# Inverse square roots as a POOL power, and four re-ordered places, in a one-core hybrid decoder trunk

## The chip, the cores and the metric

The kernel runs on one core of a Trainium2 chip. The metric is the device time of one execution in microseconds (us). TensorE (PE) does the products, VectorE (DVE), ScalarE (ACT) and GpSimd (POOL) the rest; transfers are issued from the queues of SP (SyncE), ACT and POOL.

## What is computed

Two residual layers over x of 512 tokens by 1024 features, all in float32, each layer followed by a dense squared-ReLU MLP of width 4096, and an RMSNorm at the end:

```python
for i in range(2):
    h = rmsnorm(x, norm_mix_g[i])
    h = chunked_spatial_gating(h, ...) if i == 0 else retention(h, ...)   # mixers A and B
    x = x + h
    h = rmsnorm(x, norm_ffn_g[i])
    x = x + squared_relu_mlp(h, mlp_w1[i], mlp_w2[i])
return rmsnorm(x, final_norm_g)
# rmsnorm(x, g) = x * rsqrt(mean(x*x, -1) + 1e-6) * g
```

Mixer A has one more RMSNorm over its gate half v, mixer B one for each of its four heads. So an inverse square root of a mean of squares is taken at ten places: nine times for all 512 tokens at once, as a 128x4 tile, and in the last norm for four groups of 128 tokens, each a 128x1 tile.

## The kernel before, in words

**Products.** Every float32 factor is split into a high part (a cast to the type fp32r) and a low part (the rest); a product is three passes on PE: high by high, high by low, low by high (`mm3`, L261). Weights come in as raw tiles by DMA from SP (some MLP tiles get a second matrix added by a DMA from POOL, L199). A raw tile holds two pieces; for each piece ACT casts `wH` (L220) and DVE subtracts `wL` (L227). `refill` (L246) issues this two to three pieces ahead of the products.

**Order.** The kernel writes the order out by hand: each engine executes its instructions in the order in which the program emits them. `steps` is a list of functions, one for each weight piece, run at the end (L1148). Small work is slipped behind a piece by `behind` hooks. A norm is a generator (`norm`, L348) whose stages such hooks advance: first the split of the sum of squares `ssq` into a high part on ACT and a low part on POOL (L316, L317); then two products with a matrix of ones (L325, L326), a masked sum on DVE (L329 to L331) and `rsqrt` (L295), eleven small DVE instructions, which give `r4`; then the split and spreading of `r4` over a row, and a last product that broadcasts it (L343 to L346).

**Start.** Five products of the identity with itself (L1140) come first, then the columns of the norm gains, then `x_chunk` (L449) for chunks 0 and 1 of x: four transposes into one PSUM tile, the casts of the first weight piece (L1145, L1146), `hH` (L457), `hL` (L459), and a copy to `xT` (L460). Then `v0` (L599) runs the first 512 columns of v with accumulators in four PSUM tiles of the tag `acc` (six tiles; the tag `mis` has two): for each chunk k three groups of four products (hH by wH, hH by wL, hL by wH; L619). Further chunks of x are transposed between them (`two_chunks`, L591). At its last piece (i == 3) the first norm's split is issued ahead of chunk 6's products, and its two statistics products ahead of chunk 7's. `tokens` (L394) runs the other three parts of v.

**MLP.** `dense` (L804) runs up to 4096 features in four quarters; for three of them the down products (`seven`, L719) follow, named p in a string that orders them. The last quarter's activations are split by `split_a` (L706), four at a time, the second four behind the sixth of the seven products of the third quarter (L820). Layer 0's last down quarter is `down_last` (products named dn, L840), layer 1's is the pair of `tokens` calls at L1121 (products named dt).

**End.** The last half of columns (c = 1) ends token group by token group (`ends`, L1081): twelve products for each of four groups, then `evac_last` (L1046): an add on DVE, squares with their sum on ACT, and a multiplication by the gain on POOL. `finish` (L1057) is a generator: the mean on DVE, an inverse root in eleven small DVE instructions, interleaved with the next group's work by `go`, then the two halves of the output, one on ACT (L1076), one on DVE (L1078), each followed by a DMA from SP (L1077, L1079).

Of the kernel before, what the change touches and what calls it, by code (L numbers as in the profile page):

```python
# [88 lines left out]
def trunk(ctx, tc, x, norm_mix_g, norm_ffn_g, a_w_in, a_b_in, a_v_norm_g, a_w_s, a_b_s, a_w_out,  # L89
# [48 lines left out]
    ms0 = keep.tile([P, NT], F32, name="ms0")  # L138

    keep.tile([P, 328], F32, name="fill")  # L140
# [4 lines left out]
    nc.gpsimd.memset(rows, 1.0)  # L145

# [148 lines left out]
    def rsqrt(dst, a, n, name):  # L295

        y, t = [work.tile([P, n], F32, tag=f"rs{i}_{n}", name=f"{name}_{i}", bufs=2) for i in range(2)]
        nc.vector.tensor_scalar(out=t.bitcast(I32), in0=a.bitcast(I32), scalar1=1, scalar2=None, op0=ALU.logical_shift_right)
        nc.vector.tensor_scalar(out=y.bitcast(I32), in0=t.bitcast(I32), scalar1=-1.0, scalar2=float(0x5F3759DF - (1 << 31)), op0=ALU.mult, op1=ALU.add)
        for i in range(3):  # L300
            nc.vector.tensor_mul(t, y, y)
            nc.vector.scalar_tensor_tensor(out=t, in0=t, scalar=0.5, in1=a, op0=ALU.mult, op1=ALU.mult)
            nc.vector.scalar_tensor_tensor(out=dst if i == 2 else y, in0=t, scalar=1.5, in1=y, op0=ALU.subtract, op1=ALU.mult)
# [16 lines left out]
    def stats(ssq, dst, scale, name):  # L320

        hi, lo = split(ssq, f"st_{name}", nc.gpsimd)
        yield
        ps = mis(f"st_{name}")
        nc.tensor.matmul(ps, lhsT=onesr, rhs=hi, start=True, stop=False)  # L325
        nc.tensor.matmul(ps, lhsT=onesr, rhs=lo, start=False, stop=True)  # L326
        own = tmp(f"own_{name}", "uz")
        a = work.tile([P, NT], F32, tag="ms", name=f"ms_{name}", bufs=2)
        nc.vector.tensor_tensor(out=by_token(own), in0=by_token(ps), in1=diag_mask, op=ALU.mult)  # L329
        nc.vector.tensor_reduce(out=a, in_=by_token(own), op=ALU.add, axis=mybir.AxisListType.X)  # L330
        nc.vector.tensor_scalar(out=a, in0=a, scalar1=scale, scalar2=EPS, op0=ALU.mult, op1=ALU.add)  # L331
        rsqrt(dst, a, NT, f"rs_{name}")
        yield
# [60 lines left out]
    def tokens(plist, bufs, evac, name, behind=None, last=None):  # L394

        accs = {}
        behind = behind or {}

        def one(i):
            def run(p):  # L400
                if i == 0:
                    for n in range(NT):
                        accs[n] = acc(f"{name}_{n}")
                aH, aL = bufs()
                for n in range(NT):
                    s = slice(n * P, (n + 1) * P)
                    for k in range(2):
                        kk = 2 * i + k
                        mm3(accs[n], aH[kk][:, s], aL[kk][:, s], p.hi[:, k, :], p.lo[:, k, :], kk == 0, kk == 7)
                advance()  # L410
                refill()
                if i in behind:
                    behind[i]()
                if i == 3:
                    for n in range(NT):
                        launch(evac(n, accs[n]))
            return run

        for i, p in enumerate(plist[:2] if last else plist):
            step(one(i), p)  # L420
        if last:
            step(lambda *ps: last(bufs, accs, evac, *ps), *plist[2:])
# [75 lines left out]
    def v_stats():  # L498
# [4 lines left out]
        rsqrt(rs4, a, NT, "rs_v")  # L503
# [94 lines left out]

    def v0(i):  # L599
        def run(p):  # L600
# [5 lines left out]
            for k in range(2):  # L606
# [3 lines left out]
                if i == 3:  # L610
                    prep(5 + k)
                    if k == 0:
                        squares(6, MIX)
                        squares(7, MIX)
                    next(nrm)
                wh, wl = p.hi[:, k, :], p.lo[:, k, :]
                for j, (h, w) in enumerate(((hH, wh), (hH, wl), (hL, wh))):
                    for n in range(NT):
# [3 lines left out]
            if i == 3:  # L622
                for n in range(NT):
                    launch(evac_v(0)(n, accs0[n]))
                next(nrm)
# [4 lines left out]
    tokens(vl[1], hs, evac_v(1), "v1", {1: nxt(nrm)})  # L630
    tokens(vl[2], hs, evac_v(2), "v2", {1: ws_prep})
# [172 lines left out]
    def dense(l, hooks):  # L804
# [6 lines left out]
        for q in range(3):  # L811
# [4 lines left out]
            for what in "upupupupuupuupp" if q == 2 else "upupupupupupupu":  # L816
                if what == "p":
                    products[j]()
                    j += 1
                    if q == 2 and j == 6:  # L820
# [225 lines left out]
    def evac_last(c):  # L1046
        def ev(n, ps):
# [5 lines left out]
            nc.gpsimd.tensor_tensor(out=xv, in0=xv, in1=wide[:, 512 * c : 512 * (c + 1)], op=ALU.mult)  # L1053
# [3 lines left out]
    def finish(n):  # L1057


        a = [work.tile([P, 1], F32, tag=f"fa{i}", name=f"fa{i}_{n}", bufs=2) for i in range(3)]  # L1060
        t, y = [work.tile([P, 1], F32, tag=f"fy{i}", name=f"fy{i}_{n}", bufs=2) for i in range(2)]
        nc.vector.scalar_tensor_tensor(out=a[0], in0=ssf[:, n, 1:2], scalar=1.0 / D, in1=ms0[:, n : n + 1], op0=ALU.mult, op1=ALU.add)
        yield
        nc.vector.tensor_scalar(out=t.bitcast(I32), in0=a[0].bitcast(I32), scalar1=1, scalar2=None, op0=ALU.logical_shift_right)
        nc.vector.tensor_scalar_mul(a[1], a[0], 0.25)
        nc.vector.tensor_scalar_mul(a[2], a[0], 0.0625)
        yield
        nc.vector.tensor_scalar(out=y.bitcast(I32), in0=t.bitcast(I32), scalar1=-1.0, scalar2=float(0x5F3759DF - (1 << 31)), op0=ALU.mult, op1=ALU.add)
        yield
        for i in range(3):  # L1070
            nc.vector.scalar_tensor_tensor(out=t, in0=y, scalar=a[i], in1=y, op0=ALU.mult, op1=ALU.mult)
            yield
            nc.vector.scalar_tensor_tensor(out=y, in0=t, scalar=3.0, in1=y, op0=ALU.subtract, op1=ALU.mult)
            yield
        o = [zt(f"out0{n}"), z2t(f"out1{n}")]
        nc.scalar.activation(o[0], tok[0][:, n, :], AF.Copy, scale=y)  # L1076
        nc.sync.dma_start(out=out[0, n * P : (n + 1) * P, 0:512], in_=o[0])  # L1077
        nc.vector.tensor_scalar_mul(o[1], tok[1][:, n, :], y)  # L1078
        nc.sync.dma_start(out=out[0, n * P : (n + 1) * P, 512:1024], in_=o[1])  # L1079

    def ends(bufs, accs, evac, *ps):  # L1081

        aH, aL = bufs()
        fins = []

        def go(steps):
            for _ in range(steps):
                for g in list(fins):
                    if next(g, "end") == "end":
                        fins.remove(g)  # L1090

        for n in range(NT):
# [6 lines left out]
            go(5)  # L1099
            fins.append(finish(n))  # L1100
            go(4 if n < 2 else 0)
        go(16)
# [10 lines left out]
    def load_gain():  # L1113
        nc.sync.dma_start(out=wide, in_=final_norm_g.partition_broadcast(P))
        nc.vector.tensor_scalar_mul(wide, wide, 0.125)
# [22 lines left out]
    warm = mis("warm")  # L1138
    for _ in range(5):
        nc.tensor.matmul(warm[:, 0:P], lhsT=ident, rhs=ident, start=True, stop=True)  # L1140
    columns(rows2, 0, 16)
    prep_tiles(0)
    for k in range(2):
        p = order[0]
        x_chunk(k, [lambda: nc.scalar.copy(out=p.hi[:, k, :], in_=p.raws[0].tile[:, k, :]),  # L1145
                    lambda: nc.vector.tensor_sub(out=p.lo[:, k, :], in0=p.raws[0].tile[:, k, :], in1=f32(p.hi[:, k, :]))])  # L1146
# [50 lines left out]
```

## Time and profile before

| | us |
|---|---|
| median of 3 runs (lowest, highest) | 1380.65 (1379.38, 1381.09) |
| the profiled execution's own time | 1382.22 |
| its span, first to last instruction | 1380.5 |
| PE busy in it | 1363.5 (99%) |
| DVE, ACT, POOL busy | 877.5, 567.3, 158.0 |

The profile is of one execution; its starts are in us from the span's start. A row of the timeline gives the start, the length, the engine, the line, the operation, output and inputs with their shapes, how many instructions are merged into the row, and in brackets how long the engine was idle before it and what ended that. A PE row's length holds the drain of the pipeline, so products overlap: their pace is read from the starts.

### The profile page before, as it was taken

Reading aid. Unit: us, or ns where it says so; the run is one execution under the profiler, and the core shown is the slowest. Engines: PE = TensorE matmul, PEld = TensorE weight load, DVE = VectorE, ACT = ScalarE, POOL = GpSimd, SP = SyncE. Lnnn points to the kernel's source line nnn. Section 1 sums busy time; section 2 is a strip of 40 time slices with the busy share of each in tenths; the row PEclk is TensorE's granted clock in tenths of the full one; section 3 lists DMA queues with packets and bytes.
Section 4 is the critical chain, followed back from the end, with each engine's and each line's share of the span. In section 5 each row is a group of like instructions: output and inputs, shape, how many; then the busy total and the mean of one; then the engine's idle time right before and its main releaser. Section 6 shows DMA issues by size and latency. Waiting matters only on the chain.

```text
span 1380.5 us, 15485 instructions
## 1 busy us (share of the span) xinstructions
PE 1363.5 (99%) x6180; PEld 1132.1 (82%) x6180; DVE 877.5 (64%) x1228; ACT 567.3 (41%) x812; POOL 158.0 (11%) x122
## 2 busy tenths in 40 slices
PE   8999999999999999999999999999999999999997
PEld 6888888888888888788888888888888888888875
DVE  6847756675665756676656574474594665766655
ACT  4647634334444434422333432333234544434342
POOL 3010111130100000011112100100121000100002
PEclk9999999999999999999999999999999999999999
DMA  6232222234684748233222222131127376665621
GB/s 230 93 127 71 92 92 92 92 123 139 164 208 131 200 136 183 93 117 111 69 85 63 90 92 92 61 121 62 62 92 214 92 183 182 144 192 150 155 77 61
DMA packets 115800, 166.71 MB, mean 121 GB/s; under 512 B 2880, under 2 KB 67984, under 8 KB 115472
## 3 DMA queue, kind: packets, MB, share of 16 engines
q1 hardware_dynamic: 103024, 140.55, 31.0%
q0 software_dynamic: 12672, 25.17, 10.8%
q8 instruction: 48, 0.79, 0.2%
q14 instruction: 24, 0.20, 0.0%
q10 hardware_dynamic: 32, 0.01, 0.0%
HBM read 163.62 MB, written 2.10 MB: 120 GB/s over the span
## 4 chain that ended last, share of the span: by engine, by line
PE 96%; DVE 2%; POOL 1%; ACT 0%; issue 0%; DVEq 0%; POOLq 0%; ACTq 0%
PE up L264 24%; PE g L264 6%; PE ro L264 6%; PE vv L264 6%; PE qk L264 6%; PE u L264 6%; PE o L264 6%; PE v L264 5%; PE dt L264 3%; PE dn L264 2%; PE av L264 2%; PE sm11a L264 2%; PE sm10a L264 2%; PE sm01a L264 2%; PE sm00a L264 2%; PE sm12a L264 1%
## 5 line engine op out<-in xcount | busy, mean ns | idle before, releaser
L227 DVE TENSOR_TENSOR wL<-raw,wH 128x1024 fp32r<-128x1024 f32 x235 | 300.5, 1283 | 48.9 <-issue 13.8
L220 ACT CAST wH<-raw 128x1024 fp32r<-128x1024 f32 x235 | 244.3, 1045 | 79.0 <-PE dt L264 14.3
L264 PE MATMUL up<-hH,wH 128*128 128x512 f32 x480 | 187.2, 390 | 0.2 <-ACT xtok L1042 0.2
L264 PE MATMUL up<-hL,wH 128*128 128x512 f32 x480 | 186.8, 389 | 0.0
L264 PE MATMUL up<-hH,wL 128*128 128x512 f32 x480 | 186.8, 389 | 0.0
L696 ACT ACTIVATE aF<-r 128x512 f32<-128x512 f32 x54 | 34.2, 633 | 218.2 <-DVE r L695 218.2
L695 DVE SCALAR_TENSOR_TENSOR r<-up,wide 128x512 f32<-128x512 f32 x54 | 37.4, 692 | 128.5 <-PE up L264 120.0
L264 PEld LDWEIGHTS up<-hH,wH 128*128 128x128 f32 x480 | 90.1, 188 | 19.1 <-ACT xtok L1042 0.5
L264 PEld LDWEIGHTS up<-hH,wL 128*128 128x128 f32 x480 | 90.1, 188 | 18.8
L264 PEld LDWEIGHTS up<-hL,wH 128*128 128x128 f32 x480 | 90.1, 188 | 18.7
L199 POOL DMA_DIRECT2D raw<-in_mlp_w_dram x22 | 28.7, 1306 | 391.1 <-DVE wL L227 261.1
L293 POOL TENSOR_TENSOR ssq<-ssq,sq 128x512 f32<-128x512 f32 x28 | 43.0, 1537 | 162.2 <-ACT sq L292 161.9
L227 DVE TENSOR_TENSOR wL<-more,wH 128x1024 fp32r<-128x1024 f32 x40 | 48.7, 1219 | 6.2 <-issue 4.7
L264 PE MATMUL u<-hH,wH 128*128 128x512 f32 x128 | 50.6, 395 | 0.0
L264 PE MATMUL g<-hH,wH 128*128 128x512 f32 x128 | 50.5, 395 | 0.0
L264 PE MATMUL o<-yH,wH 128*128 128x512 f32 x128 | 50.4, 394 | 0.0
L264 PE MATMUL ro<-ryL,wH 128*128 128x512 f32 x128 | 50.0, 391 | 0.0
L264 PE MATMUL qk<-hH,wH 128*128 128x512 f32 x128 | 50.0, 391 | 0.0
L264 PE MATMUL vv<-wH,hH 128*128 128x512 f32 x128 | 50.0, 391 | 0.0
L264 PE MATMUL ro<-ryH,wH 128*128 128x512 f32 x128 | 50.0, 390 | 0.0
L264 PE MATMUL ro<-ryH,wL 128*128 128x512 f32 x128 | 50.0, 390 | 0.0
L264 PE MATMUL g<-hH,wL 128*128 128x512 f32 x128 | 49.9, 390 | 0.0
(394 smaller groups left out, 3087.2 us busy)
## 6 DMA issues: line engine op xcount, KB each, us to landing
raw<-in_mlp_w_dram SPq DMA_DIRECT2D x50, 1024.0 KB, 5.2
raw<-in_b_w_in_dram SPq DMA_DIRECT2D x24, 1024.0 KB, 5.1
raw<-in_mlp_w_dram POOLq DMA_DIRECT2D x22, 1024.0 KB, 9.1
more<-in_mlp_w_dram SPq DMA_DIRECT2D x20, 1024.0 KB, 5.1
raw<-in_a_w_in_dram SPq DMA_DIRECT2D x14, 1024.0 KB, 5.1
raw<-in_a_w_out_dram SPq DMA_DIRECT2D x8, 1024.0 KB, 5.0
raw<-in_b_w_out_dram SPq DMA_DIRECT2D x8, 1024.0 KB, 5.0
raw<-in_a_w_in_dram SPq DMA_DIRECT2D x8, 256.0 KB, 6.6
```

The costliest lines, as they stand in the source:

```text
L199: nc.gpsimd.dma_start(out=r.tile, in_=src, accum_op=ALU.add)
L220: nc.scalar.copy(out=p.hi, in_=p.src)
L227: nc.vector.tensor_sub(out=p.lo, in0=p.src, in1=f32(p.hi))
L264: nc.tensor.matmul(ps, lhsT=a, rhs=b, start=start and i == 0, stop=stop and i == 2, skip_group_check=resumed)
L293: nc.gpsimd.tensor_tensor(out=state["ssq"], in0=state["ssq"], in1=sq, op=ALU.add)
L695: nc.vector.scalar_tensor_tensor(out=r, in0=ps, scalar=0.0, in1=rbc, op0=ALU.max, op1=ALU.mult)
L696: nc.scalar.activation(a, r, AF.Square)
```

## The change

- `rsqrt` becomes one POOL instruction: the tile to the power of a tile `mhalf` that holds -0.5.
- The second chunk's transposes, casts and copies (`first_chunk(1)`) are issued behind the first four products of chunk 0 instead of ahead of them; two more products of the identity follow the first chunk's transposes.
- In `v0`'s last piece the split of the first norm is issued ahead of chunk 7's products, and the statistics products behind them. The second part of v takes two of its accumulators from `mis`, and the broadcast of `r4` moves behind the third part's first piece.
- The second `split_a` of a layer moves behind the seventh product.
- At the end the c = 1 half is no longer multiplied by the gain on POOL: one DVE instruction takes the sum, the root and the gain together. Its DMA goes from SP, that of the other half from ACT. Each group's way out is issued whole behind its products. The gain's multiplication by 0.125 goes.

```diff
+    mhalf = keep.tile([P, NT], F32, name="mhalf")
-    keep.tile([P, 328], F32, name="fill")
+    keep.tile([P, 320], F32, name="fill")
+    nc.gpsimd.memset(mhalf, -0.5)
...
-    def rsqrt(dst, a, n, name):
-        y, t = [work.tile([P, n], F32, tag=f"rs{i}_{n}", name=f"{name}_{i}", bufs=2) for i in range(2)]
...
-        for i in range(3):
-            nc.vector.tensor_mul(t, y, y)
...
+    def rsqrt(dst, a, n):
+        nc.gpsimd.tensor_tensor(out=dst, in0=a, in1=mhalf[:, 0:n], op=ALU.pow)
...
-    def tokens(plist, bufs, evac, name, behind=None, last=None):
+    def tokens(plist, bufs, evac, name, behind=None, last=None, banks=(acc,) * 4):
...
-                        accs[n] = acc(f"{name}_{n}")
+                        accs[n] = banks[n](f"{name}_{n}")
...
+    def first_chunk(k):
+        p = order[0]
+        x_chunk(k, [lambda: nc.scalar.copy(out=p.hi[:, k, :], in_=p.raws[0].tile[:, k, :]),
+                    lambda: nc.vector.tensor_sub(out=p.lo[:, k, :], in0=p.raws[0].tile[:, k, :], in1=f32(p.hi[:, k, :]))])
...
                     if k == 0:
                         squares(6, MIX)
                         squares(7, MIX)
-                    next(nrm)
+                    else:
+                        next(nrm)
                 for j, (h, w) in enumerate(((hH, wh), (hH, wl), (hL, wh))):
+                    if kk == 0 and j == 1:
+                        first_chunk(1)
...
             if i == 3:
+                next(nrm)
                 for n in range(NT):
                     launch(evac_v(0)(n, accs0[n]))
                 next(nrm)
...
-    tokens(vl[1], hs, evac_v(1), "v1", {1: nxt(nrm)})
-    tokens(vl[2], hs, evac_v(2), "v2", {1: ws_prep})
+    tokens(vl[1], hs, evac_v(1), "v1", banks=(acc, acc, mis, mis))
+    tokens(vl[2], hs, evac_v(2), "v2", {0: nxt(nrm), 1: ws_prep})
...
-                    if q == 2 and j == 6:
+                    if q == 2 and j == 7:
                         do(lambda: [split_a(l, i) for i in range(4, 8)])
...
             if c == 0:
                 nc.vector.tensor_scalar(out=ms0[:, n : n + 1], in0=ssf[:, n, 0:1], scalar1=1.0 / D, scalar2=EPS, op0=ALU.mult, op1=ALU.add)
-            nc.gpsimd.tensor_tensor(out=xv, in0=xv, in1=wide[:, 512 * c : 512 * (c + 1)], op=ALU.mult)
+                nc.gpsimd.tensor_tensor(out=xv, in0=xv, in1=wide[:, 0:512], op=ALU.mult)
...
     def finish(n):
+        a, y = [work.tile([P, 1], F32, tag=f"f{i}", name=f"f{i}_{n}", bufs=2) for i in "ay"]
+        nc.vector.scalar_tensor_tensor(out=a, in0=ssf[:, n, 1:2], scalar=1.0 / D, in1=ms0[:, n : n + 1], op0=ALU.mult, op1=ALU.add)
+        rsqrt(y, a, 1)
         o = [zt(f"out0{n}"), z2t(f"out1{n}")]
+        nc.vector.scalar_tensor_tensor(out=o[1], in0=tok[1][:, n, :], scalar=y, in1=wide[:, 512:D], op0=ALU.mult, op1=ALU.mult)
+        nc.sync.dma_start(out=out[0, n * P : (n + 1) * P, 512:1024], in_=o[1])
         nc.scalar.activation(o[0], tok[0][:, n, :], AF.Copy, scale=y)
+        nc.scalar.dma_start(out=out[0, n * P : (n + 1) * P, 0:512], in_=o[0])
...
     def load_gain():
         nc.sync.dma_start(out=wide, in_=final_norm_g.partition_broadcast(P))
-        nc.vector.tensor_scalar_mul(wide, wide, 0.125)
...
+    warm_up(5)
     columns(rows2, 0, 16)
     prep_tiles(0)
+    first_chunk(0)
+    warm_up(2)
```

The eleven-instruction chain of `finish`, its generator steps and the loop over chunks 0 and 1 ahead of `steps` go.

## Rows read from the trace of the kernel before

**Rows 1.** The page's first part: busy time, share of the span, instructions.

```profile
PE 1363.5 (99%) x6180; PEld 1132.1 (82%) x6180; DVE 877.5 (64%) x1228; ACT 567.3 (41%) x812; POOL 158.0 (11%) x122
```

**Rows 2.** Waits of PE, longest first: waiter, releaser, us, times, longest.

```profile
PE xt L452 <- DVE hL L459: 2.2, 1, 2.2
...
PE up L264 <- ACT xtok L1042: 0.2, 1, 0.2
```

**Rows 3.** Timeline of the start: PE, DVE and ACT around the first two chunks.

```profile
4.06 1.11 PE L452 MATMUL xt<-ident,xr 128*128 128x128 f32 x4
...
5.22 0.75 DVE L457 TENSOR_SCALAR hH<-xt,gT 128x512 fp32r<-128x512 f32 x1 [0.87 <-PE xt L452]
...
7.32 0.59 ACT L460 COPY xT<-xt 128x512 f32<-128x512 f32 x1 [1.89 <-DVE hL L459]
...
7.37 1.09 PE L452 MATMUL xt<-ident,xr 128*128 128x128 f32 x4 [2.19 <-DVE hL L459]
...
8.11 2.06 PE L619 MATMUL v<-wH,hH 128*128 128x512 f32 x4
...
9.96 1.91 PE L619 MATMUL v<-wL,hH 128*128 128x512 f32 x4
...
13.20 1.03 PE L452 MATMUL xt<-ident,xr 128*128 128x128 f32 x8
```

**Rows 4.** DMA issues from 1.8 to 2.0 us (chunk 1 of x, issued at 1.83): KB, landing.

```profile
xr<-in_x_dram SPq DMA_DIRECT2D x1, 256.0 KB, 5.4
```

**Rows 5.** Timeline of the first statistics: PE's last groups of chunk 6, the split, chunk 7.

```profile
30.82 1.07 PE L619 MATMUL v<-wL,hH 128*128 128x512 f32 x4
...
31.73 1.07 PE L619 MATMUL v<-wH,hL 128*128 128x512 f32 x4
...
32.95 1.28 POOL L317 TENSOR_TENSOR st_mix<-ssq,st_mix 128x512 fp32r<-128x512 f32 x1 [0.73 <-ACT st_mix L316]
...
34.28 0.50 PE L326 MATMUL st_mix<-st_mix,onesr 128*128 128x512 f32 x1 [0.86 <-POOL st_mix L317]
...
34.62 1.08 PE L619 MATMUL v<-wH,hH 128*128 128x512 f32 x4
```

**Rows 6.** Timeline at the end of layer 0's seventh product: the late splits, dn's first products.

```profile
580.38 2.49 DVE L714 TENSOR_TENSOR aL<-aF,aH 128x512 fp32r<-128x512 f32 x4
...
582.93 0.39 PE L264 MATMUL dn0a<-aL,wH 128*128 128x512 f32 x1
...
584.05 0.50 PE L264 MATMUL dn0a<-aH,wL 128*128 128x512 f32 x1 [0.74 <-DVE wL L227]
```

**Rows 7.** Timeline of the same place in layer 1: dt's first products.

```profile
1325.27 0.39 PE L264 MATMUL dt<-wH,aH 128*128 128x512 f32 x1
...
1326.58 0.50 PE L264 MATMUL dt<-wL,aH 128*128 128x512 f32 x1 [0.93 <-DVE wL L227]
```

**Rows 8.** Timeline of the end: first group's add and mean, last group's add, last DMA.

```profile
1362.05 0.69 DVE L1049 TENSOR_TENSOR xtok<-xtok,dt 128x512 f32<-128x512 f32 x1 [7.11 <-PE dt L264]
...
1363.59 0.16 DVE L1062 SCALAR_TENSOR_TENSOR fa<-ssf,ms 128x1 f32<-128x1 f32 x1 [0.85 <-ACT fsq L1050]
...
1370.21 0.69 DVE L1049 TENSOR_TENSOR xtok<-xtok,dt 128x512 f32<-128x512 f32 x1
...
1377.05 0.39 SPq L1079 DMA_DIRECT2D out_dram<-out  x1
```

**Rows 9.** Groups of POOL instructions by line and shape: busy us, mean ns, idle before.

```profile
L1053 POOL TENSOR_TENSOR xtok<-xtok,wide 128x512 f32<-128x512 f32 x8 | 10.3, 1286 | 81.4 <-ACT fsq L1050 81.4
...
L477 POOL TENSOR_SCALAR vgh<-gT 128x16 f32<-128x16 f32 x1 | 0.2, 243 | 0.0
```

**Rows 10.** Timeline: a three-operand DVE instruction on SBUF tiles of 128x512.

```profile
14.98 0.75 DVE L284 SCALAR_TENSOR_TENSOR hL<-xT,gT,hH 128x512 fp32r<-128x512 f32 x1
```

**Rows 11.** Timeline, POOL and DVE at layer 0's MLP norm: queued DMA, root's last instruction.

```profile
318.62 1.46 POOL L199 DMA_DIRECT2D raw<-in_mlp_w_dram  x1 [10.90 <-DMA raw<-in_mlp_w_dram]
...
318.76 0.16 DVE L303 SCALAR_TENSOR_TENSOR r<-rs_ffn,rs_ffn 128x4 f32<-128x4 f32 x1
```

More of the change, by code (lines that the diff above doesn't have):

```diff
@@ L293, in squares @@
             nc.gpsimd.tensor_tensor(out=state["ssq"], in0=state["ssq"], in1=sq, op=ALU.add)
-    def rsqrt(dst, a, n, name):
-        y, t = [work.tile([P, n], F32, tag=f"rs{i}_{n}", name=f"{name}_{i}", bufs=2) for i in range(2)]
-        nc.vector.tensor_scalar(out=t.bitcast(I32), in0=a.bitcast(I32), scalar1=1, scalar2=None, op0=ALU.logical_shift_right)
-        nc.vector.tensor_scalar(out=y.bitcast(I32), in0=t.bitcast(I32), scalar1=-1.0, scalar2=float(0x5F3759DF - (1 << 31)), op0=ALU.mult, op1=ALU.add)
-        for i in range(3):
-            nc.vector.tensor_mul(t, y, y)
-            nc.vector.scalar_tensor_tensor(out=t, in0=t, scalar=0.5, in1=a, op0=ALU.mult, op1=ALU.mult)
-            nc.vector.scalar_tensor_tensor(out=dst if i == 2 else y, in0=t, scalar=1.5, in1=y, op0=ALU.subtract, op1=ALU.mult)
+    def rsqrt(dst, a, n):
+        nc.gpsimd.tensor_tensor(out=dst, in0=a, in1=mhalf[:, 0:n], op=ALU.pow)
     def over_tokens(v):
@@ L331, in stats @@
         nc.vector.tensor_scalar(out=a, in0=a, scalar1=scale, scalar2=EPS, op0=ALU.mult, op1=ALU.add)
-        rsqrt(dst, a, NT, f"rs_{name}")
+        rsqrt(dst, a, NT)
         yield
@@ L502, in v_stats @@
         nc.vector.tensor_scalar(out=a, in0=s, scalar1=0.25 / GW, scalar2=EPS, op0=ALU.mult, op1=ALU.add)
-        rsqrt(rs4, a, NT, "rs_v")
+        rsqrt(rs4, a, NT)
         nc.vector.tensor_scalar_mul(rs4, rs4, 0.5)
@@ L1057, in finish @@
     def finish(n):
[L1060 to L1074, printed above, removed]
+        a, y = [work.tile([P, 1], F32, tag=f"f{i}", name=f"f{i}_{n}", bufs=2) for i in "ay"]
+        nc.vector.scalar_tensor_tensor(out=a, in0=ssf[:, n, 1:2], scalar=1.0 / D, in1=ms0[:, n : n + 1], op0=ALU.mult, op1=ALU.add)
+        rsqrt(y, a, 1)
         o = [zt(f"out0{n}"), z2t(f"out1{n}")]
+        nc.vector.scalar_tensor_tensor(out=o[1], in0=tok[1][:, n, :], scalar=y, in1=wide[:, 512:D], op0=ALU.mult, op1=ALU.mult)
+        nc.sync.dma_start(out=out[0, n * P : (n + 1) * P, 512:1024], in_=o[1])
         nc.scalar.activation(o[0], tok[0][:, n, :], AF.Copy, scale=y)
-        nc.sync.dma_start(out=out[0, n * P : (n + 1) * P, 0:512], in_=o[0])
-        nc.vector.tensor_scalar_mul(o[1], tok[1][:, n, :], y)
-        nc.sync.dma_start(out=out[0, n * P : (n + 1) * P, 512:1024], in_=o[1])
+        nc.scalar.dma_start(out=out[0, n * P : (n + 1) * P, 0:512], in_=o[0])
     def ends(bufs, accs, evac, *ps):
         aH, aL = bufs()
[L1084 to L1090, printed above, removed]
         for n in range(NT):
@@ L1098, in ends @@
             launch(evac(n, accs[n]))
[L1099 to L1102, printed above, removed]
+            finish(n)
     tt = {2: [(0, 0), (0, 1)], 3: [(0, 2)], 4: [(0, 3)], 5: [(1, 0)], 6: [(1, 1)], 7: [(1, 2), (1, 3)]}
@@ L1136, in trunk, with warm_up @@
     load_a()
-    warm = mis("warm")
-    for _ in range(5):
-        nc.tensor.matmul(warm[:, 0:P], lhsT=ident, rhs=ident, start=True, stop=True)
+    def warm_up(n):
+        warm = mis("warm")
+        for _ in range(n):
+            nc.tensor.matmul(warm[:, 0:P], lhsT=ident, rhs=ident, start=True, stop=True)
+    warm_up(5)
     columns(rows2, 0, 16)
     prep_tiles(0)
[L1143 to L1146, printed above, removed]
+    first_chunk(0)
+    warm_up(2)
     pos["piece"] = pos["low"] = raws[0].split = 1
```

## The prediction, on record before the changed kernel ran

> **What bounds the kernel now.** The page's first part first: PE is busy for 99% of the span, DVE for 64%, ACT for 41%, POOL for 11% [rows 1]. So a shorter instruction on DVE, ACT or POOL is worth nothing by itself; it counts where PE stands still, or before PE's first and behind PE's last product. The waits of PE come next: six entries in all, of which the longest is 2.2 us, at the start, and the shortest 0.2 us [rows 2]. PE's ends are modelled, so I then read the starts in the timeline, where a stall shows as a gap above the usual pace: four 128x512 products start 0.91 us after the four before (30.82 to 31.73, [rows 5]), 0.2275 us each, 2.73 us for a group of twelve and 5.46 us for a piece of 24. Four places stand out, and the change touches each.
>
> **The start.** Chunk 0's transposes start at 4.06, its hH is written at 5.22 + 0.75 = 5.97, and PE's next instruction, chunk 1's transposes, starts at 7.37 [rows 3]. The releaser shown is hL, but chunk 1 of x, issued at 1.83, landed 5.4 us later at 7.2 [rows 4]: either alone would hold PE. From 8.11 the first four products take 1.85 us (to 9.96), and the eight after them 3.24 us (to 13.20): 0.46 and 0.41 us each, about half the pace of rows 5 (1.2 GHz for 2.4), though the granted clock of the view reads full there. PE had worked at half pace, then idled before 7.37.
>
> The change puts the first four products ahead of chunk 1's transposes. Chunk 0's transposes end at 5.2, two more identity products fill about 1 us (estimate: the transposes' 0.27 us for each of their four passes), so the four start at about 6.2. They end at 8.05 at half pace. Chunk 1's transposes then wait for nothing new: x landed at 7.2; if they take the PSUM tile of chunk 0, they wait for its copy to xT, 7.32 + 0.59 = 7.91 [rows 3]. At half pace throughout (transposes 1.09, eight products 3.24) the next transposes start at 12.4 instead of 13.20: 0.8 us gained. At full pace from the first product on (transposes 8.0 to 8.5, eight at 0.2275) they start at 10.3: 2.9 us. Between them the pace doubles at about 9 us: 8.05 + 1.09 + 1.82 = 11.0, **2.2 us**, which I take, since PE now works without the pause of 5.2 to 7.4 and the old kernel, restarted at 7.4, doubled its pace by 13.2. The Trainium skill (TensorE: Matmul & The Clock Gate, Part 1) says that half rate is the default and that sustained work releases the clock; by that rule the unbroken work from the warm-up on would release it earlier and the term would lie near 2.9, by the rows alone it may stay at 0.8. Trace and rule agree on the half pace at the start. Behind this point hH, hL and weights of chunk 1 follow its transposes as before, with nothing else queued between.
>
> **The first statistics.** Chunk 6's products end at 31.73 + 0.91 = 32.64 on PE's pace; chunk 7's start at 34.62, because the low half of the split is written on POOL until 32.95 + 1.28 = 34.23 [rows 5]. Of the 1.98 us the two statistics products need 2 x 0.2275. Behind chunk 7's products (2.73 us) they find the split done: 32.64 + 2.73 = 35.4 against 34.23. **1.5 us** go. If POOL's chain does not move forward with the start, the margin of 1.1 us shrinks by the 2.2 gained there, and up to 1 us stays. Late next is r4, and with it the evacuation of the four first accumulators. The next part no longer waits for these (two tiles of acc, two of mis, the second of which DVE's masked sum frees 0.7 us behind the statistics); the third part asks for them four pieces, 21.8 us, later. On DVE the evacuation holds the third piece's wL: from the statistics to its end stand eight passes over 512 columns at 0.69 [rows 8], wL itself, twice as wide, 1.4, and small ones, some 0.8, together 7.7 us, against the two pieces that are ready, 10.9: the power may take 3.2 us there.
>
> **The late splits.** At layer 0's first dn products the starts go 582.93, 584.05: 1.12 - 0.23 = **0.9 us** lost to wL, which stands on DVE behind four subtractions of 2.49 us from 580.38 [rows 6]. In layer 1, the first product starts at 1325.27 and the second, the first that reads wL, at 1326.58: 1.31 - 0.23 = **1.1 us** [rows 7]. Moved behind the seventh product, the four leave wL 2.5 us earlier, more than either stall. What they feed comes late next: dn's second half of chunks starts 24 products, 5.46 us, after the seventh product; before it DVE has two adds of 0.69 [rows 8] and the 2.49, 3.9 us. A margin of 1.5 us; in layer 1 it is a piece more. No DMA moves with this step.
>
> **The end.** Before: the last group's add starts at 1370.21, the last DMA is issued at 1377.05 [rows 8], and the span ends 3.45 us later, at 1380.5. After: for each group, add, squares and mean take 1363.59 + 0.16 - 1362.05 = 1.70 us [rows 8], then the power p with 0.07 us of handing over on either side (estimate from the steps between engines in rows 5 and 8), then the three-operand product, 0.75 [rows 10], and 0.03: 2.62 + p. All are in order on DVE, so the next group's add stands behind this group's wait for POOL. PE gives a group every 2.73 us, so for p over 0.1 this loop sets the end: last issue at 1362.05 + 3 x (2.62 + p) + 1.70 + 0.14 + p + 0.75 + 0.05 = 1372.55 + 4p. The other half (ACT, with its DMA now from ACT) runs beside it. No row shows a power. The nearest below is POOL's smallest arithmetic, 0.243 us for 128x16, the nearest above its ordinary pass over 128x512, 1.286 [rows 9]: 1373.5 to 1377.7, a gain of 3.5 or a loss of 0.7. With one to four elements it is nearer to the small one: p = 0.4, 1374.15, **2.9 us**. The Trainium skill (GPSIMD Engine Reference, 2.1) says that the first call of newly loaded POOL code costs about 6 us more; no row here shows such a call. By it (an estimate) the first norm's power would be late, 2.8 us of it beyond the 3.2 that are covered, and the sum 5.8 instead of 8.6; the end's four powers would not be touched.
>
> **Edits at nothing.** The other nine roots take eleven small instructions each from DVE; none of PE's six waits lies behind one, so they give nothing. At layer 0's MLP norm POOL's queue holds a DMA that waits for its raw tile until 318.62 and takes 1.46; the power, if issued behind it, writes r4 at about 320.5, not at 318.92 [rows 11], 1.6 us late; the broadcast is a piece (5.46 us) away. The gain's scaling leaves DVE, whose wait was covered by two pieces ready.
>
> **The sum.** 2.2 + 1.5 + 0.9 + 1.1 + 2.9 = 8.6 us off the span of 1380.5: 1371.9. The profiled execution took 1382.2, 1.6 above the median of 1380.65; the parts are the same in any run, so 1380.65 - 8.6 = **1372.0**. A measurement can tell about 0.2%, 2.8 us.
>
> **Rivals.**
> - **The power is slow at each call** and becomes the bound of the end, the other side. Place: the three-operand product on DVE, which waits for the power, with the next group's add behind it, four times in a row. Price: 4p - 4.5 at the end against 5.7 gained elsewhere; equal at p = 2.55, slower by more than 2.8 from p = 3.25. At 5 us: 15.5 - 5.7, and 1.8 at the first norm: 1392. For it: the operation is in no row, POOL's plain passes are slow. Against: it has one element per partition, where a pass has 512 in 1.286. Chance 0.06; between 1.85 and 3.25 no change can be told, 0.05.
> - **The power is slow once**, at its first call behind the first statistics: it costs PE p - 3.2 there, decides from 3.2 on, and costs the end nothing; were it 6 us, 2.8 would be lost: 1374.8. No row speaks for it or against it. Chance 0.08. (The first-call rule of the GPSIMD Engine Reference in the Trainium skill, above, is this case.)
> - **Only half arrives**: the pace at the start doubles no earlier (0.8) and p is 0.9 (the end gains 0.9): 5.2 in all, 1375.4. For it: rows 3 show half pace long after work resumed. 0.14.
> - **The moved splits do not do what they are moved for**: dn's second half waits in place of its first; the 2.0 us stay, 1374.0. Against: the margins above. 0.05.
> - The forecast, 0.62.
>
> **Range and chances.** The best ends (2.9 at the start, p = 0.24) give 10.0 off, 1370.6; a run's spread of 1 us below that. Above, the third rival with a margin. 1369.4 to 1376.2 leaves out the first rival and a little on each side. Faster 0.89, the same 0.05, slower 0.06.
>
> **What would show it.** Right: in the new profile the four first products start near 6.2, chunk 7's 0.9 us behind chunk 6's last four, no gap in dn and dt, the last add within 1 us of PE's last product, POOL's power well under 1 us, the last issue some 4 us behind PE's last product. Wrong: products at half pace beyond 12 us, PE waiting for mis tiles in v's second part, DVE idle for POOL at the end longer than its own work.

## The result and the profile after

The changed kernel takes 1372.82 us (median of 4 runs, 1372.59 to 1373.16) against 1380.87 of the kernel before in the same comparison (1379.38 to 1381.10): ratio 0.9944, 95% interval 0.9927 to 0.9961. It is 8.05 us faster. A later comparison of the two gave 1372.86 and 1380.52, with the same ratio and interval. The profiled execution took 1372.68 us over a span of 1371.0, so it lies at its median; the profiled one of before lay 1.4 us above its own. The two spans therefore differ by 9.5 us, more than the medians do, and the 1.4 has to be found too.

The page's first part, which answers to [rows 1], and the waits of PE, which answer to [rows 2]:

```profile
PE 1360.9 (99%) x6184; PEld 1131.5 (83%) x6184; DVE 856.5 (62%) x1088; ACT 566.7 (41%) x812; POOL 166.5 (12%) x132
...
PE warm L1121 <- POOL ident masks.py:199: 1.4, 1, 1.4
PE up L266 <- ACT xtok L1047: 0.2, 1, 0.2
PE v L266 <- DVE wL L229: 0.2, 1, 0.2
```

PE's waits for chunk 1, the statistics, dn and dt are gone; one of 0.2 us is new.

**The start**, which answers to [rows 3]:

```profile
4.97 1.06 PE L1121 MATMUL warm<-ident 128*128 128x128 f32 x4
...
6.12 1.37 PE L623 MATMUL v<-wH,hH 128*128 128x512 f32 x4
...
7.32 0.58 ACT L456 COPY xT<-xt 128x512 f32<-128x512 f32 x1 [2.50 <-DVE hL L455]
7.33 0.60 PE L448 MATMUL xt<-ident,xr 128*128 128x128 f32 x4
...
7.68 1.18 PE L623 MATMUL v<-wL,hH 128*128 128x512 f32 x4
...
9.62 1.03 PE L448 MATMUL xt<-ident,xr 128*128 128x128 f32 x8
```

The first four products start at 6.12 and take 1.21 us; the next eight take 7.68 to 9.62, 0.24 each, where [rows 3] has 0.41. Chunk 2's transposes start at 9.62, not 13.20: 3.6 us gained in this pair. Chunk 1's transposes start beside the copy to xT at 7.32 and do not wait for it.

**The first statistics** ([rows 5]):

```profile
28.12 1.07 PE L623 MATMUL v<-wH,hL 128*128 128x512 f32 x4
29.03 1.07 PE L623 MATMUL v<-wH,hH 128*128 128x512 f32 x4
29.29 2.23 POOL L313 TENSOR_TENSOR st_mix<-ssq,st_mix 128x512 fp32r<-128x512 f32 x1 [0.74 <-ACT st_mix L312]
...
32.24 0.40 PE L266 MATMUL v<-wH,hH 128*128 128x512 f32 x1
...
34.21 1.03 POOL L299 TENSOR_TENSOR r<-ms_mix,mhalf 128x4 f32<-128x4 f32 x1 [2.69 <-DVE ms_mix L327]
35.27 2.73 DVE L487 SCALAR_TENSOR_TENSOR vz<-v,r,bvb 128x512 f32<-128x512 f32 x4 [1.14 <-POOL r L299]
...
40.07 2.49 DVE L477 SCALAR_TENSOR_TENSOR vs<-vs,vz 128x512 f32<-128x512 f32 x4
42.47 1.22 DVE L229 TENSOR_TENSOR wL<-raw,wH 128x1024 fp32r<-128x1024 f32 x1
43.16 0.39 PE L266 MATMUL v<-wH,hH 128*128 128x512 f32 x1
43.75 0.50 PE L266 MATMUL v<-wL,hH 128*128 128x512 f32 x1 [0.20 <-DVE wL L229]
```

Chunk 7 stands 0.91 behind chunk 6, at PE's pace. From chunk 6's last group to v's second part it is 32.24 - 28.12 = 4.12 us; before, 5.63 (31.73 in [rows 5] to 37.36): 1.5 gained. The first product of that part in the kernel before:

```profile
37.36 0.39 PE L264 MATMUL v<-wH,hH 128*128 128x512 f32 x1
```

The new wait: the third piece's wL ends at 43.69, behind the evacuation, and PE loses 43.75 - 43.16 - 0.23 = 0.36 us.

**The late splits** ([rows 6, 7]): dn's first products start 0.23 and 0.22 us apart, dt's 0.23.

```profile
578.13 0.39 PE L266 MATMUL dn0a<-aH,wH 128*128 128x512 f32 x1
...
578.36 0.39 PE L266 MATMUL dn0a<-aL,wH 128*128 128x512 f32 x1
...
578.58 0.39 PE L266 MATMUL dn0a<-aH,wL 128*128 128x512 f32 x1
579.27 2.49 DVE L719 TENSOR_TENSOR aL<-aF,aH 128x512 fp32r<-128x512 f32 x4
...
1319.37 0.39 PE L266 MATMUL dt<-wH,aH 128*128 128x512 f32 x1
...
1319.60 0.39 PE L266 MATMUL dt<-wL,aH 128*128 128x512 f32 x1
```

**The end** ([rows 8]), and POOL's powers by shape (columns as in [rows 9]):

```profile
1354.93 0.69 DVE L1054 TENSOR_TENSOR xtok<-xtok,dt 128x512 f32<-128x512 f32 x1 [7.10 <-PE dt L266]
...
1362.66 0.39 PE L266 MATMUL dt<-wH,aL 128*128 128x512 f32 x1
1363.91 0.68 DVE L1054 TENSOR_TENSOR xtok<-xtok,dt 128x512 f32<-128x512 f32 x1
...
1366.20 0.75 DVE L1068 SCALAR_TENSOR_TENSOR out<-xtok,fy,wide 128x512 f32<-128x512 f32 x1 [0.66 <-POOL fy L299]
...
1366.95 0.37 ACTq L1071 DMA_DIRECT2D out_dram<-out  x1
...
L299 POOL TENSOR_TENSOR r<-ms_ffn,mhalf 128x4 f32<-128x4 f32 x2 | 3.1, 1544 | 0.0
L299 POOL TENSOR_TENSOR fy<-fa,mhalf 128x1 f32<-128x1 f32 x4 | 2.2, 554 | 19.2 <-DVE fa L1065 19.2
L299 POOL TENSOR_TENSOR r<-ms_mix,mhalf 128x4 f32<-128x4 f32 x2 | 2.1, 1030 | 9.7 <-DVE ms_mix L327 9.7
```

A power on one element per partition takes 0.55 us, on four 1.03, and 1.54 at the two MLP norms; the first of the program, at 34.21, takes 1.03, the mean of its two. The adds come 2.99 us apart on average, (1363.91 - 1354.93) / 3, so the loop through POOL does set the end, at a little above PE's 2.73. From PE's last product to the end of the span it is 8.34 us (1362.66 to 1371.0), 10.71 before (1369.79 to 1380.5): 2.4 gained. The last product of the kernel before:

```profile
1369.79 0.39 PE L264 MATMUL dt<-wH,aL 128*128 128x512 f32 x1
```

The ledger of the profiled pair, by the starts of the same products: start 3.6, statistics 1.5, the new wL wait and small changes in v's parts -0.5, dn 1.0, dt 1.2, the end 2.4, and 0.3 scattered: 9.5 us.

### The profile page after: what moved, and what is told of

It is laid out like the page before. It is cut to its first block, busy times and chain, and to the rows that moved or that the text cites. A ratio compares the mean times of both kernels' runs of the same rounds, so it can differ in the third digit from the quotient of the medians.

```text
span 1371.0 us, 15352 instructions
## 1 busy us (share of the span) xinstructions
PE 1360.9 (99%) x6184; PEld 1131.5 (83%) x6184; DVE 856.5 (62%) x1088; ACT 566.7 (41%) x812; POOL 166.5 (12%) x132
## 4 chain that ended last, share of the span: by engine, by line
PE 95%; DVE 2%; DMA 1%; issue 0%; ACT 0%; POOL 0%; SPq 0%; POOLq 0%; DVEq 0%; ACTq 0%
PE up L266 24%; PE g L266 6%; PE ro L266 6%; PE vv L266 6%; PE qk L266 6%; PE u L266 6%; PE o L266 6%; PE v L266 4%; PE dt L266 3%; PE dn L266 2%; PE av L266 2%; PE sm11a L266 2%; PE sm10a L266 2%; PE sm01a L266 2%; PE sm00a L266 2%; PE sm12a L266 2%
## 5 line engine op out<-in xcount | busy, mean ns | idle before, releaser
L266 PE MATMUL vv<-wL,hH 128*128 128x512 f32 x128 | 49.9, 390 | 0.0
```

What stands on the lines that cost most here:

```text
L266: nc.tensor.matmul(ps, lhsT=a, rhs=b, start=start and i == 0, stop=stop and i == 2, skip_group_check=resumed)
```

## The experiments

Unless an entry says otherwise, the edit is made to the changed kernel, and times stand against its 1372.8. A range in brackets is the lowest and the highest run, and behind a ratio (to the kernel before) its 95% interval. Two readings are used throughout: the start of chunk 2's transposes, and the span less this start, which is the whole rest of the kernel.

**No extra identity products.**

```
     first_chunk(0)
-    warm_up(2)
```

> The changed kernel without the two extra identity products behind chunk 0's transposes. Theory (the start's 3.6 us come from the pace: unbroken work lets PE reach full pace near 7 us): PE then idles about 0.9 us ahead of the first four products, which still start near 6.1; the pace doubles later, so chunk 2's transposes start 0.5 to 2.5 us later than 9.62, and the kernel is slower than the changed one by as much. Rival (the order alone does it): chunk 2's transposes start at 9.6 within 0.2 and the time does not move (1372.8 within 0.4).

1374.4 us (1373.7 to 1374.6), ratio 0.9954 (0.9939 to 0.9969).

```profile
6.12 2.04 PE L623 MATMUL v<-wH,hH 128*128 128x512 f32 x4 [0.94 <-DVE hH L453]
...
10.41 1.10 PE L623 MATMUL v<-wH,hL 128*128 128x512 f32 x4
...
11.35 1.04 PE L448 MATMUL xt<-ident,xr 128*128 128x128 f32 x8
```

The order is the same, PE only idles from 5.2 to 6.1, and the products run at half pace until 10.3. The two products are worth 1.6 us.

**The old order, with the extra products.**

```
-                    if kk == 0 and j == 1:
-                        first_chunk(1)
...
     warm_up(2)
+    first_chunk(1)
```

> The changed kernel with chunk 1's transposes back ahead of the first four products, the two identity products kept. Theory (order and pace both count): PE idles from 6.1 until chunk 1 of x has landed at 7.2; the first four products start at 8.1 or later and chunk 2's transposes at 10.5 to 12.5 instead of 9.62, so 1 to 3 us slower than the changed kernel. Rival (the warm-up alone does it): at full pace from 7.3 on, transposes 0.55 and twelve products 2.73, chunk 2's transposes at 10.7, 1.1 us slower; and if the pace alone mattered less than 0.5.

1372.9 us (1372.6 to 1375.2), ratio 0.9948 (0.9933 to 0.9963): no difference, and my theory that the order carries part of the start falls. Chunk 1's transposes wait 0.3 us for x, which landed at 6.2, and chunk 2's start at 9.55, against 9.62.

**The start as before: old order, no extra products.**

```
-                    if kk == 0 and j == 1:
-                        first_chunk(1)
...
     first_chunk(0)
-    warm_up(2)
+    first_chunk(1)
```

> The changed kernel with its start as in the kernel before: no extra identity products, and chunk 1's transposes ahead of the first products of the weights; statistics, splits and end stay changed. If the extra products carry the start and the order is worth about 1.9 us without them (the run without the products had chunk 2's transposes at 11.35 against 13.20 before), the time is 1372.8 + 3.6 = about 1376.4. If the order is worth nothing even without the products, it is the 1374.4 of the run without them. Chunk 2's transposes begin near 13.2 in the one case and 11.4 in the other.

1374.5 us (1373.9 to 1374.6), ratio 0.9955 (0.9943 to 0.9968), the same as without the products in the new order. So the order is worth nothing in either case, and the whole start, undone, costs 1.6 us and not 3.6.

```profile
5.89 1.09 PE L448 MATMUL xt<-ident,xr 128*128 128x128 f32 x4 [0.71 <-DMA xr<-in_x_dram]
...
11.46 1.03 PE L448 MATMUL xt<-ident,xr 128*128 128x128 f32 x8
```

This is the order of the kernel before; there chunk 1's transposes started at 7.37 [rows 3]. They start here while DVE still has hL to write (6.48 to 7.22): hL never held them. What differs is when chunk 1 of x lands, 5.7 here and 7.2 in [rows 4], from an issue at the same time.

**Only the two products, in the kernel before.**

```
+        if k == 0:
+            more = mis("warm")
+            for _ in range(2):
+                nc.tensor.matmul(more[:, 0:P], lhsT=ident, rhs=ident, start=True, stop=True)
```

> The kernel before with one thing added: two 128-column products of the identity behind the transposes of chunk 0 of x, and nothing else of the change. If those products alone carry the gain of the start (3.6 us of chunk 2's transposes, 13.20 to 9.62), chunk 2's transposes begin near 9.6 to 9.9 here, the first four products of a step last 1.0 to 1.2 us instead of 2.0, and the time is 1380.6 - 3.6 = about 1377.0. If the start needs the products and the new order together, chunk 2's transposes begin near 11.4 and the time is about 1378.7. If the products do nothing in the old order, 1380.6.

1379.4 us against 1380.65, ratio 0.9995 (0.9986 to 1.0004), which can't be told from no change. Its eleven runs lie at two levels, seven at 1379.3 to 1379.4 and four at 1380.5 to 1380.9. The kernel before has the lower level too, in two of its fifteen runs beside these, so the products may make it more frequent; so few runs don't settle it. In the profiled one, of the upper level, chunk 1's transposes still wait 0.5 us for x behind the extra products, the first four products take 1.85 us at half pace, and chunk 2's start at 11.30. That is between the cases that I had written down; it does not show that the products suffice in the old kernel.

**The kernel before, and the changed one, a second time.** Nothing is edited.

> The kernel before, unchanged, profiled a second time, to see how much of the 3.6 us between the two starts was chance. If the late landing of chunk 1 of x (7.2 us) belonged to that one execution, chunk 1's transposes start near 5.9 to 6.6 here, chunk 2's near 11.5, and the span is 1.5 to 1.7 us shorter, near 1378.9. If it belongs to the kernel, they start at 7.4 and 13.2 again and the span is 1380.5.

> The changed kernel, unchanged, profiled a second time. If the moment at which the pace doubles is the same in every execution, chunk 2's transposes start at 9.6 again. If it varies from one execution to the next, they start anywhere from 9.4 to 11.4, as in the kernels of the other runs that share its start, and the span follows by as much: 1370.8 to 1372.8. Median 1372.8.

The kernel before:

```profile
6.51 1.09 PE L452 MATMUL xt<-ident,xr 128*128 128x128 f32 x4 [1.34 <-DMA xr<-in_x_dram]
...
12.47 1.04 PE L452 MATMUL xt<-ident,xr 128*128 128x128 f32 x8
```

The changed kernel:

```profile
6.11 1.16 PE L623 MATMUL v<-wH,hH 128*128 128x512 f32 x4
...
9.41 1.03 PE L448 MATMUL xt<-ident,xr 128*128 128x128 f32 x8
```

The kernel before: x landed at 6.4, and the releaser shown is now the DMA. The span is 1379.8, 0.7 shorter than in the first profile, as chunk 2's transposes start 0.73 earlier; that is half of what I had expected of this case, since the pace doubled only at the last of chunk 0's twelve products, at 12.4, where the old start above doubled it at 10.9. The changed kernel: 1372.86 us (1372.56 to 1373.16), span 1370.9. The span less the start of chunk 2's transposes shows what is chance:

| kernel | chunk 1 of x lands | first clock entry | chunk 2's transposes | span | difference |
|---|---|---|---|---|---|
| before | 7.2 | 12.98 | 13.20 | 1380.5 | 1367.3 |
| before, again | 6.4 | 12.38 | 12.47 | 1379.8 | 1367.3 |
| before, two products | 6.4 | 9.82 | 11.30 | 1378.8 | 1367.5 |
| changed | 5.8 | 6.55 | 9.62 | 1371.0 | 1361.4 |
| changed, again | 6.9 | 5.77 | 9.41 | 1370.9 | 1361.5 |
| old order | 6.2 | 6.18 | 9.55 | 1370.9 | 1361.4 |
| no extra products | 6.5 | 10.27 | 11.35 | 1372.6 | 1361.3 |
| old start | 5.7 | 10.93 | 11.46 | 1372.7 | 1361.2 |

The third column is the start of the first entry that the trace holds on TensorE's granted clock. The entry reads full, and the pace of the products doubles at the same moment. Ahead of it the trace has no entry, and the views show such a stretch as full; this is the full clock beside the half pace in the prediction.

Behind the start the profiled executions of each kernel repeat to 0.3 us: 1367.4 before, 1361.4 after, a gain of 6.0. Their scatter sits in the first 13 us. In the last comparison the runs of before had a median span of 1378.8, so their chunk 2 started near 1378.8 - 1367.3 = 11.5; the four of the changed kernel had 1371.15, which gives 9.75 (both worked out, not seen). The start is worth about 1.75 at these medians, and the other 1.8 of the 3.6 belong to the pair that was profiled first: 0.7 to the late landing, and about 1.0 (12.47 against 11.5) to a pace that doubled late in the kernel before.

**The statistics as before.** Chunk 7 again behind both statistics products, v's second part on four tiles of acc, r4 behind its second piece.

```
-                    else:
-                        next(nrm)
+                    next(nrm)
...
             if i == 3:
-                next(nrm)
...
-    tokens(vl[1], hs, evac_v(1), "v1", banks=(acc, acc, mis, mis))
-    tokens(vl[2], hs, evac_v(2), "v2", {0: nxt(nrm), 1: ws_prep})
+    tokens(vl[1], hs, evac_v(1), "v1", {1: nxt(nrm)})
+    tokens(vl[2], hs, evac_v(2), "v2", {1: ws_prep})
```

> The changed kernel with the first norm's stages, v's second part's accumulators and the broadcast of r4 where they stood before; the root stays a power. Theory (the stall of 1.5 us returns, the new wait of 0.36 us in v's second part goes): first products of v's second part 1.5 us later than 32.24, the time about 1.1 us above the changed kernel's, 1373.9. Rival (POOL's chain moved forward with the start, so the split is ready): less than 0.3 us. Other rival (the power, slower to come back than the old chain, makes the second part wait for its accumulators): 2 us or more.

1374.95 us (1374.6 to 1376.6), ratio 0.9961 (0.9947 to 0.9975), some 1 us more than expected. PE waits 1.4 us for the split on POOL, the wait for wL is gone, and from chunk 6's last group to v's second part it is 5.88 us against 4.12. Span 1373.9 less a start of 11.42 is 1362.5: 1.1 above the changed kernel, as expected. The rest is its start, whose products ran at half pace until 10.4 although the extra products are in place:

```profile
PE st_mix L322 <- POOL st_mix L313: 1.4, 1, 1.4
...
6.12 2.07 PE L622 MATMUL v<-wH,hH 128*128 128x512 f32 x4
```

Even the fastest of its five runs, 1374.62, stands 0.7 above 1372.8 + 1.1, so the start seems to have been late in all of them. The edit changes no instruction ahead of chunk 6's products, at 26 us; why they were late is open.

**The late splits as before.**

```
-                    if q == 2 and j == 7:
+                    if q == 2 and j == 6:
```

> The changed kernel with the second half of the last splits back behind the sixth product in both layers. Theory: the gaps at dn's and dt's first reads of wL return, 1.0 and 1.2 us, time 1375.0. Rival (the rest of the change has moved DVE's work so that they are covered): under 0.5 us in all.

1375.1 us (1374.8 to 1375.5), ratio 0.9960 (0.9946 to 0.9975). Both stalls are back:

```profile
PE dt L266 <- DVE wL L229: 1.0, 1, 1.0
PE dn0a L266 <- DVE wL L229: 0.7, 1, 0.7
```

Span less start: 1373.0 - 9.41 = 1363.6, 2.2 above.

**Nine roots as a chain on DVE** (`rsqrt_dve` is the old eleven-instruction chain).

```
-        rsqrt(dst, a, NT)
+        rsqrt_dve(dst, a, NT)
...
-        rsqrt(rs4, a, NT)
+        rsqrt_dve(rs4, a, NT)
```

> The changed kernel with the nine norms' roots back as eleven DVE instructions; the four at the end stay powers. Theory (PE hides all but the first): v's second part waits for wL 0.36 us now with 1.26 us from the mean to r4; the chain takes 2.2, so the wait grows by about 0.9 us; all else unchanged: 1373.7. Rival (DVE's freed time matters at the norms of both layers): slower by 2 us or more. Other rival: no difference within 0.3.

1373.1 us (1373.05 to 1373.6), ratio 0.9947 (0.9933 to 0.9960): within the scatter of the changed kernel. The wait shows the mechanism all the same:

```profile
PE v L266 <- DVE wL L229: 1.3, 1, 1.3
```

It was 0.2 to 0.3. Span less start: 1371.4 - 9.41 = 1362.0, 0.6 above, where 0.9 was expected.

**The end's roots as a chain on DVE.**

```
-        rsqrt(y, a, 1)
+        rsqrt_dve(y, a, 1)
```

> The changed kernel with the end's four roots as eleven DVE instructions, whole, in place of the power. Theory (one loop of add, squares, mean, root, output on DVE sets the end): 2.2 us in place of 0.75 with both hand-overs, so each of the four rounds of the loop takes 1.4 us more and the last DMA is issued 5 to 6 us later: 1378.5. Rival (only the last group's root lies on the path, PE's 2.73 us a group hide the others): 1.5 us, 1374.3.

1378.3 us (1377.6 to 1378.6), ratio 0.9982 (0.9973 to 0.9991). Between the three-operand products at the end it is (1371.75 - 1358.38) / 3 = 4.46 us, against (1366.20 - 1357.32) / 3 = 2.96. The power carries the new end: with the chain in the same order the time is 5.4 us longer (span less start: 1376.4 - 10.05 = 1366.4, 5.0 longer). The power in the old order of the end was not run.

**Both halves of the output from SP's queue.**

```
-        nc.scalar.dma_start(out=out[0, n * P : (n + 1) * P, 0:512], in_=o[0])
+        nc.sync.dma_start(out=out[0, n * P : (n + 1) * P, 0:512], in_=o[0])
```

> The changed kernel with both halves' DMAs issued from SP. Theory (the second issue waits 0.4 us behind the first, as it did before): the end 0.2 to 0.4 us later. Rival (the two DMAs, issued at once, held each other up: from the last issue to the end 4.05 us here against 3.45 before): no later, or up to 0.3 us earlier.

1373.15 us (1372.8 to 1373.6), ratio 0.9946 (0.9933 to 0.9960): not to be told from no change, so the time does not tell theory from rival. The trace shows both at work:

```profile
1367.65 0.38 SPq L1071 DMA_DIRECT2D out_dram<-out  x1
...
out_dram<-out SPq DMA_DIRECT2D x4, 256.0 KB, 2.2
```

The last issue comes 0.7 later, 0.4 of it because it stands behind the other half's, but the span ends 3.45 us behind it (1371.1), not 4.05.

**A version that takes up what the traces still show.** The first half of the last splits moves from ahead of the sixth product to behind it, the second stays behind the seventh; in v's second part the next wL is taken ahead of the pending evacuation; at the end each group's output stands behind the next group's add.

```
-                    if q == 2 and j == 7:
-                        do(lambda: [split_a(l, i) for i in range(4, 8)])
+                    if q == 2 and j >= 6:
+                        do(lambda h=4 * (j - 6): [split_a(l, i) for i in range(h, h + 4)])
...
-                    if q == 2 and i == 8:
-                        do(lambda: [split_a(l, i) for i in range(4)])
...
+                if early and i == 0:
+                    refill()
                 advance()
...
         rsqrt(y, a, 1)
+        yield
...
-            finish(n)
+            next(fin, None)
+            fin = finish(n)
+            next(fin)
+        next(fin, None)
```

> The changed kernel with three more moves: both halves of the last splits one product later (behind the sixth and the seventh), the next weight piece's wL ahead of the pending evacuation in v's second part, and at the end each group's output behind the next group's add. Theory: the wait of 0.36 us in v's second part goes, the gap of some 0.5 us at the seventh product's second group of products goes in both layers, and the last add starts 0.9 us sooner after PE's last product: 2.2 us off, 1370.6. Rival (the splits, later, make dn's and dt's first products wait again): 1 to 2 us of it lost, 1372 to 1373.

1370.2 us (1369.7 to 1370.5), ratio 0.9923 (0.9910 to 0.9937), 2.6 us better than the changed kernel, where 2.2 was expected.

```profile
PE warm L1126 <- POOL ident masks.py:199: 1.4, 1, 1.4
PE up L266 <- ACT xtok L1047: 0.2, 1, 0.2
...
1361.46 0.39 PE L266 MATMUL dt<-wH,aL 128*128 128x512 f32 x1
...
1361.89 0.69 DVE L1054 TENSOR_TENSOR xtok<-xtok,dt 128x512 f32<-128x512 f32 x1 [1.08 <-PE dt L266]
...
1365.11 0.34 ACTq L1072 DMA_DIRECT2D out_dram<-out  x1
```

The wait for wL is gone; by the starts of the same products 0.5 us goes at the seventh product in layer 0 and 0.6 in layer 1; and at the end the adds keep PE's pace (the last stands 0.43 behind PE's last product, 1.25 in the changed kernel), so the last issue comes 3.65 us behind that product instead of 4.3. Span less start: 1368.8 - 10.22 = 1358.6, 2.8 below.

## Why the prediction was right, and where its steps were not

The forecast of 1372.0 us stands 0.8 below the measured 1372.8, in its range and on its side. Its steps one by one:

- **The start, 2.2 us.** The size is near right at the medians (1.6 by the undone start, 1.75 by the spans of the later comparison, 2.05 by what the 6.0 behind the start leave of 8.05), the reading of the rows was not. "Either alone would hold PE" fell: it was the landing of chunk 1 alone, and 0.8 us of it (7.2 against 6.4) belonged to that execution. So "the parts are the same in any run" was the step that failed: the profiled time lay above the median because of this very part, and 2.2 was near right for a usual start, not for the one it was read from. That it comes so near is in part luck, since it was worked out from the landing and the pace of that one execution.

  Two smaller points fell too: chunk 1's transposes do not wait for the copy to xT, and the full pace came at 6.55 and 5.77 in the two profiles of the changed kernel, not at 9. The work that fills the pause brings it forward: with PE idle from 5.2 to 6.1 the products stayed at 1.2 GHz's pace until 10.3, with the gap filled they ran at that of 2.4 GHz from some moment between 5.0 and 7.9 in eight of ten profiles. It is not enough by itself: in the other two, with the same products, the pace doubled at 10.4 (the old statistics) and 9.8 (the kernel before), and what sets the moment stays open.

  By the rule of the Trainium skill quoted there (TensorE: Matmul & The Clock Gate, Part 1) the term would have lain near 2.9; the traces agree with it that work brings the full pace, but the gains measured (1.6 to 2.05) lie below that term. The Trainium skill (the same page and part) says that this moment varies from run to run of one kernel. The traces agree: in eight profiles with the changed kernel's start it came between 5.0 and 10.4, in three in the old order without extra products between 10.9 and 13.0.
- **The first statistics, 1.5 us.** Right, 1.5, but 0.4 to 0.5 comes back as the wait for wL. The step that was mis-sized is "together 7.7 us, against the two pieces that are ready": the sum left out the four passes of L477, 2.49 us. With them 7.7 + 2.5 + 1.0 for the power is 11.2 against 10.9, and the wait follows. (The trace has about 9.4 us of passes and 1.9 us in which DVE waits, for the power and for ACT's cast of r4.) That the power's latency counts there is shown by the nine roots on DVE: the wait grew by 1.0. The margin at the split was 0.5 us and not 1.1, as POOL's pass took until 31.52 and PE needed it at 32.00.
- **The late splits, 0.9 + 1.1 us.** Right: 1.0 and 1.2 in the ledger, 2.2 in the run that undoes them, and dn's second half did not wait.
- **The end, 2.9 us.** The loop through POOL sets it, as worked out, with p at 0.55 instead of 0.4. The last issue is 4.3 us behind PE's last product, as forecast (4.36), but by luck: the slower power adds 0.6, and the hand-overs overlap more than I had counted (2.99 us for a loop where 2.62 + 0.55 = 3.17), which takes 0.7 off. One sign was set wrong: the last add stands 1.25 us behind PE's last product, not within 1, and the forecast's own sum, 1362.05 + 3 x 3.02 - 1369.79, gives 1.3. What is missing is behind it: 4.05 us from the last issue to the end of the span, 3.45 before and again 3.45 with both DMAs from SP: two halves that start at once on two queues land later. I had counted the earlier issue alone; this is the term that was mis-sized. Gain 2.4.
- **The nine other roots at nothing.** Not to be told from that at the medians (0.3), though not for the reason given: beside the moved statistics one root does stand ahead of a wL that PE waits for.
- **The rivals.** The power at 0.55 us, 1.54 at most on four elements, excludes the slow power, and 1.03 us at its first call excludes the case of slow once: the first-call rule of the Trainium skill (GPSIMD Engine Reference, 2.1) does not show in this kernel. The moved splits did what they were moved for.

The gain was forecast at 8.6 and is 8.05, with 6.0 of it behind the start, where 6.4 was forecast, and 2.05 in it, where 2.2 was. In the later comparison the gain is 7.66; by the spans the start was worth 1.75 there. The remaining 0.2 of the 0.8 is the median of before, 1380.87 in the comparison for 1380.65.

## What to carry to other kernels

Before a wait in one profile is priced, see whether it is the same in a second execution: here the span less the start of one early instruction was constant to 0.3 us, and the scatter of the profiled executions was the landing of one DMA and the moment at which PE's pace doubled. When counting what an engine has to do before a deadline, list every pass between the two points from the trace, not from memory of the stage: one left-out group of 2.5 us was a new wait. A loop between engines that is longer than PE's step, as the 2.99 us against 2.73 here, sets the pace; moving the consumer behind the next producer's step, as in the last version, hid it.

## What was unexpected of the hardware

- Chunk 1 of x, the same 256 KB issued 1.81 to 1.83 us into the span, took between 3.9 and 5.7 us to land in the fourteen profiles: 5.7 with the old statistics, 3.9 with the old start, though neither edit changes anything ahead of its issue. What sets it is open.
- The pass on POOL that splits the first sums took 1.28 us before [rows 5] and 2.23 in the changed kernel, beside DVE's wL:

```profile
29.16 3.44 DVE L229 TENSOR_TENSOR wL<-raw,wH 128x1024 fp32r<-128x1024 f32 x2
```

  DVE's two passes took 1.72 us each there, and 1.22 at 42.47. The Trainium skill (GPSIMD Engine Reference, 1. Specifications) says that POOL contends with DVE for SBUF where a DVE instruction has two inputs there; both inputs of wL are in SBUF, and the traces agree. This was not tried by itself.
- A power took 0.55 us for one element per partition and 1.02 to 1.05 for four, but 1.54 at the two MLP norms; in layer 0 its record starts 0.5 us before the DMA issue ahead of it on POOL ends (314.92 against 315.40), and what lengthens it was not tried. From the first two sizes alone, an estimate is 0.16 us for each element on 0.4.
- Output DMAs of 256 KB that start at once on two queues landed 2.6 to 3.3 us after their issue (below, the last two groups of the changed kernel), and 2.0 to 2.6 one behind the other on SP's. In the last version's first three groups, where SP's and ACT's issues stand 0.7 us apart, both land in 2.0 to 2.1: it is the start at once that costs, not the second queue.

```profile
out_dram<-out ACTq DMA_DIRECT2D x2, 256.0 KB, 2.8
out_dram<-out SPq DMA_DIRECT2D x2, 256.0 KB, 2.6
```
